# Moving the second plain pair of the two-stream FFN ahead of the operand sums, and dealing the modulation sums to other places

## The chip, the cores and the metric

The kernel runs on one core of one Trainium2 chip. The metric is device microseconds of one execution; lower is better. The time of the kernel before is 2478.84 us, the median of three runs (2477.21 to 2480.55).

## The reference

All data is fp32. A sequence of 256 rows of 1024 columns goes through a first block of two layers (a mixing stage, then a feed-forward network with a short convolution). Its output and a second sequence `ctx` of 256 rows then go through a second block of two layers. The part that the change touches is the half-step FFN of the second block, whose gain and shift come from a conditioning vector:

```
m  = (silu(cond) @ w_mod + b_mod).reshape(9, 1024)        # modulation: 9 rows of 1024
def ffn_half_step(s, m, i, norm_g, w_in, w_out):
    h  = rmsnorm(s, norm_g) * (1 + m[3*i+1]) + m[3*i]
    gu = h @ w_in                                         # 1024 x 5632
    y  = (silu(gu[:, :2816]) * gu[:, 2816:]) @ w_out      # 2816 x 1024
    return s + 0.5 * m[3*i+2] * y

for l in range(2):
    x, ctx = ffn_half_step(x, m_x, 0, ..), ffn_half_step(ctx, m_c, 0, ..)
    x, ctx = mixing stage over both
    x      = ffn_half_step(x, m_x, 2, ..)
    if l == 0:
        ctx = ffn_half_step(ctx, m_c, 2, ..)
```

So three times both streams pass through one FFN with the same weights (`ffn2s`: layer 0 step 0, layer 0 step 2, layer 1 step 0), and the last FFN works on x alone (`ffn2`).

## The kernel before, in words

**Products.** TensorE takes operands in a reduced-precision type, so each fp32 operand is split into a part `hi` (a cast on ScalarE, L303) and a part `lo` (the difference on VectorE, L304). A product then takes three matmuls, hi·hi, hi·lo, lo·hi (`mm3`, L308 to L310). Weights are split in the same way, as they arrive: `upraw` is the tile that the DMA fills, `upwhi` and `upwlo` are its two parts. A suffix in a tile's name is its phase: `f` is the first part of an FFN, `t` the operand sums, `up` the up projection, `dn` the down projection, `e` the last FFN, `lat`, `cv` and `wo` the mixing stage.

**Two-stream FFN, `ffn2s`.** The up projection makes 22 pairs (gate column block, up column block) for both streams. The first `NU` = 3 pairs are plain: `firsts` issues 24 matmuls for each of four results of a pair (two halves, two streams). They run on unnormalised rows; `plain` then reads the results out of PSUM, multiplies them by the row factor of each stream (`rooted`, L1088 and L1091), and applies Silu and the product (L1237, L1238). Pairs 3 and on take seven products in place of eight, in the manner of Strassen (`begin`, `middle`, `ends`). For those, `sums` builds the operands from the normalised rows of both streams: for each k of 0 to 3 it scales and normalises a row tile of x and one of ctx (L1119, L1120, L1122), forms four sums and differences (L1135, L1136, L1138, L1143) and splits all of them into hi and lo. The operands are called x1, x2, t1 to t4 and c2. `seven` loads the raw weights of a pair, adds them on DMA queues and on VectorE (L1164) and splits the four sums that it needs.

**PSUM.** There are three pools: `ps` with four banks, `sc` with two and `tp` with two. In the first part pair 0 takes three `ps` banks; pair 1 takes both `sc` banks and the fourth `ps` bank; pair 2 takes the three `ps` banks of pair 0 again. The first seven-product pair, j = 3, takes a `ps` bank for its first result (`upps`, W11·x1), one for W12·x2, and an `sc` bank for s1·t1 (`upsc`). So it needs banks that pair 1 held.

**Modulation sums.** `mod_step(n)` does up to n of a list of row sums that later stages need. Each is one pass of VectorE over 1024 columns (L473), and every second one first loads 512 KB of `w_mod` (tile `wm`, on SP's queue). Calls of it are spread through the loops over pairs j. What is left on the list is done where the next stage needs it (`mod_in`).

**What sets the order.** A scheduler orders the program on each engine by priority and readiness, and each engine then runs its instructions strictly in that order. `tc.issue_after(x)` orders what is written inside it behind x. Tile pools hand out buffers in rotation, so who frees a buffer also decides when a load starts. The lines that matter before:

```
        g0 = self.plain(first[0], Rs, gmore(0))
        self.phase = "t"
        self.sums(Rs, tmore)
        ...
                    g.append(self.plain(first[j], Rs_in, gmore(jj)) if j else g0)
        ...
                u = self.begin(a[wu][l, 2 * j], a[wu][l, 2 * j + 1])
                self.mod_step(1 + (n > 0 and jj % 2))
```

Pair 0 is read out of PSUM ahead of the sums, pairs 1 and 2 behind them.

Of the kernel before, what the change touches and what calls it, by code (L numbers as in the profile page):

```python
# [216 lines left out]
class Net:  # L217
# [740 lines left out]
    def ffn1(self, l, R):  # L958
# [9 lines left out]
        for j in range(KF):  # L968
            if j % 2 == 0:
                pair = self.r4(2, 2, T)  # L970
            us = []
            for i in range(2):
                if j:
                    ps = self.times(W if 2 * j + i == 2 else a["w1u"][l, 2 * j + i], h)
                else:
                    ps = self.f1()
                    nc.vector.tensor_tensor(ps, first[i], R, ALU.mult)  # L977
                if i == 0 and (j % 2 if l == 1 else j > 9):
                    self.mod_step(1, (0, 1, 16))
                c = KF * i + j  # L980
                u = self.f1()
                nc.scalar.activation(u, ps, AF.Identity, bias=self.c1(l, "fb", c), scale=self.c1(l, "fw", 44 + c))
                nc.vector.scalar_tensor_tensor(u[:, 1:T], ps[:, 0:T - 1], self.c1(l, "fw", c), u[:, 1:T],
                                               ALU.mult, ALU.add)
                nc.vector.scalar_tensor_tensor(u[:, 0:T - 1], ps[:, 1:T], self.c1(l, "fw", 88 + c), u[:, 0:T - 1],
                                               ALU.mult, ALU.add)
                us.append(u)
            s = self.f1()
            act = nc.scalar.activation(s, us[0], AF.Silu)
            if l == 0 and j == 8:  # L990
                with self.tc.issue_after(act.ins):
                    nc.scalar.activation(self.cond, self.cond, AF.Silu)
            nc.vector.tensor_tensor(s, s, us[1], ALU.mult)
            self.parts(pair[:, j % 2, 0, :], pair[:, j % 2, 1, :], s)
            g.append((pair[:, j % 2, 0, :], pair[:, j % 2, 1, :]))
# [112 lines left out]
    def sums(self, Rs, more):  # L1108
# [3 lines left out]
        self.B7 = {n: [] for n in ("x1", "x2", "c2", "t1", "t2", "t3", "t4")}  # L1112
        tiles = (self.r4(1024, more=m) for m in more)

        def h(s, k):

            f = self.f2().rearrange("p (a b) -> p a b", a=2)
# [13 lines left out]
        for k in range(4):  # L1131
# [9 lines left out]
                y = next(tiles).rearrange("p (a h b) -> p a h b", a=2, h=2)  # L1141
            t4 = self.f1()
            nc.vector.scalar_tensor_tensor(t4, c[:, 0], -1.0, x[:, 1], ALU.mult, ALU.subtract)  # L1143
            self.parts(y[:, k % 2, 0], y[:, k % 2, 1], t4)
            self.B7["t4"].append((y[:, k % 2, 0], y[:, k % 2, 1]))

    def seven(self, gate, up):
# [4 lines left out]
        s = self.t("es", [P, 1024], 2, pool=self.p_second).rearrange("p (a b) -> p a b", a=8)  # L1152
        W = {}

        def split(x, a, b=None):
            n = x.shape[1]
            hi, lo = [self.t(t, [P, 1024], 4, F32R)[:, :n * P].rearrange("p (a b) -> p a b", a=n)
                      for t in ("whi", "wlo")]
# [84 lines left out]
    def ffn2s(self, l, step, Rs, tmore, gmore, n4):  # L1243
# [6 lines left out]
        if self.mods and self.mods[0][3]:  # L1250

            self.mod_step(1)
        g0 = self.plain(first[0], Rs, gmore(0))
        self.phase = "t"
        self.sums(Rs, tmore)
        out = [{}, {}]
# [1 line left out]
        for n, (j0, j1) in enumerate(CHUNKS):  # L1258
            g, todo = [], []
            self.phase = "up"  # L1260
            for jj, j in enumerate(range(j0, j1)):
                if j < NU:
                    g.append(self.plain(first[j], Rs_in, gmore(jj)) if j else g0)
                    continue
                u = self.begin(a[wu][l, 2 * j], a[wu][l, 2 * j + 1])
                self.mod_step(1 + (n > 0 and jj % 2))
                if todo:
                    todo.pop(0)()
                self.middle(u, todo.pop(0) if todo else lambda: None)
# [36 lines left out]
    def ffn2(self, l, step, R, nh, ng):  # L1306
# [10 lines left out]
        for half in range(2):  # L1317
            g = []
            for jj in range(HF):
                j = half * HF + jj  # L1320
                if j >= nu:
                    pss = []
                    for i in range(2):
                        pss.append(self.times(W if 2 * j + i == 2 * nu else a[wu][l, 2 * j + i], h))
                        self.mod_step(1)
                s = self.f2()[:, :T]
                if j >= nu:
                    nc.scalar.activation(s, pss[0], AF.Silu)
# [369 lines left out]
    def body(self):  # L1698
# [18 lines left out]
        with tc.tile_pool(name="second", bufs=1) as big:  # L1717
# [6 lines left out]
            for l in range(LAYERS):  # L1724
                self.next = two("w2i", l)

                if l == 0:
                    Rs = self.ffn2s(l, 0, Rs, [False] * 14, lambda jj: jj > 0, 8)
                else:
                    Rs = self.ffn2s(l, 0, Rs, [i >= 7 for i in range(14)], lambda jj: jj == 0, 8)  # L1730
                self.next = two("w2u2", l)
                Rs = self.mix2(l, Rs)
                if l == 0:
# [28 lines left out]
```

## Time and profile before

| what | before |
|---|---|
| median of three runs | 2478.84 us |
| the profiled execution | 2478.33 us |
| its span on the core | 2476.4 us, mean granted clock 0.99 |
| TensorE matmul busy | 2405.1 us, 97% of the span |
| VectorE busy | 2081.4 us, 84% |
| ScalarE busy | 1407.3 us, 57% |

The busy share is a mean over all stages. The gap of 1.9 us between the profiled execution and its span lies outside the records. Times in the views count from the start of the span. In a timeline a row is one instruction, or several of one kind run together (x2, x4): start, time until the last one's end, engine, line, operation, tiles, and in brackets the idle time ahead of it with what ended it. Matmuls overlap, so that the distance of two starts, and not the listed duration, is what one matmul takes.

### The profile page before, as it was taken

What the parts mean: (1) busy time and instruction counts of PE and PEld (TensorE: products, weight loads), DVE (VectorE), ACT (ScalarE), POOL (GpSimd) and SP (SyncE); (2) the same over time, 40 slices, a digit from 0 to 9 for tenths busy, and PEclk for the clock granted to TensorE, in tenths of its full rate; (3) what the DMA queues carried; (4) which work ended last, traced back from release to release, by engine and by line L of the source; (5) the groups of instructions that cost most, each with busy time, mean ns of one, the idle gap of its engine ahead of it and who ended that gap; (6) DMA issues with size and microseconds to landing.
All of it is one profiled execution on the core that took longest, in us unless ns stands there. A gap on an engine that the chain in (4) does not pass through costs nothing.

```text
span 2476.4 us, 45471 instructions
## 1 busy us (share of the span) xinstructions
PE 2405.1 (97%) x17419; PEld 2240.9 (90%) x17419; DVE 2081.4 (84%) x3779; ACT 1407.3 (57%) x2529; POOL 100.0 (4%) x128
## 2 busy tenths in 40 slices
PE   8999999999999989999999989999989999999998
PEld 7999999899899988989887888989888989888998
DVE  7888997988999787889877788888888889888754
ACT  7766665756665563535536673535563535667444
POOL 0000000000000000100000000101010101000000
PEclk9999999999999999999999999999989999999999
DMA  7545667545676556777331347777447778434664
GB/s 250 171 154 181 214 215 259 179 157 166 219 227 212 173 137 196 198 206 205 121 107 35 117 128 211 185 216 205 152 108 208 199 232 247 135 110 155 217 206 122
DMA packets 145195, 441.68 MB, mean 178 GB/s; under 512 B 16720, under 2 KB 19536, under 8 KB 144720
## 3 DMA queue, kind: packets, MB, share of 16 engines
q1 hardware_dynamic: 128560, 408.88, 51.0%
q0 software_dynamic: 16416, 29.89, 7.4%
q8 instruction: 137, 2.24, 0.4%
q14 instruction: 82, 0.67, 0.1%
HBM read 437.66 MB, written 1.05 MB: 177 GB/s over the span
## 4 chain that ended last, share of the span: by engine, by line
PE 79%; DVE 10%; DMA 5%; ACT 3%; issue 2%; SPq 0%; DVEq 0%; ACTq 0%; POOLq 0%
PE upps L310 7%; PE upps L308 7%; PE upps L309 7%; PE dnps L308 6%; PE dnps L310 6%; PE dnps L309 6%; DMA upes<-in_w2u 3%; DVE upwlo L304 2%; PE eps L308 2%; PE eps L310 2%; PE eps L309 2%; PE upsc L308 1%; PE upsc L309 1%; PE upsc L310 1%; DVE upjunk L473 1%
## 5 line engine op out<-in xcount | busy, mean ns | idle before, releaser
L303 ACT CAST upwhi<-upraw 128x1024 fp32r<-128x1024 f32 (+1 forms) x253 | 241.0, 953 | 199.6 <-PE upps L309 82.7
L304 DVE TENSOR_TENSOR upwlo<-upraw,upwhi 128x1024 fp32r<-128x1024 f32 (+1 forms) x253 | 274.3, 1100 | 26.9 <-ACT upwhi L303 25.2
L310 PE MATMUL upps<-tr,upwlo 128*128 128x256 f32 x931 | 264.6, 284 | 10.5 <-DVE upwlo L304 10.3
L308 PE MATMUL upps<-tr,upwhi 128*128 128x256 f32 x931 | 265.1, 285 | 0.9 <-ACT upf L1202 0.9
L309 PE MATMUL upps<-tr,upwhi 128*128 128x256 f32 x931 | 263.9, 284 | 0.0
L303 ACT CAST dnwhi<-dnraw 128x896 fp32r<-128x896 f32 (+3 forms) x146 | 130.8, 897 | 205.1 <-PE dnps L309 145.8
L310 PEld LDWEIGHTS upps<-tr,upwlo 128*128 128x128 f32 x931 | 178.1, 191 | 12.5 <-DVE upwlo L304 12.5
L310 PE MATMUL upps<-hr,upwlo 128*128 128x256 f32 x656 | 184.5, 282 | 1.2 <-DVE upwlo L304 1.1
L308 PE MATMUL upps<-hr,upwhi 128*128 128x256 f32 x656 | 185.0, 282 | 0.2 <-DVE upf L977 0.2
L309 PE MATMUL upps<-hr,upwhi 128*128 128x256 f32 x656 | 185.1, 282 | 0.0
L308 PEld LDWEIGHTS upps<-tr,upwhi 128*128 128x128 f32 x931 | 178.2, 191 | 4.4 <-ACT upf L1208 3.0
L309 PEld LDWEIGHTS upps<-tr,upwhi 128*128 128x128 f32 x931 | 178.1, 191 | 0.3
L304 DVE TENSOR_TENSOR dnwlo<-dnraw,dnwhi 128x896 fp32r<-128x896 f32 (+3 forms) x146 | 150.1, 1030 | 23.6 <-ACT dnwhi L303 22.8
L310 PE MATMUL dnps<-upr,dnwlo 128*128 128x256 f32 (+1 forms) x535 | 169.6, 317 | 0.0
L308 PE MATMUL dnps<-upr,dnwhi 128*128 128x256 f32 (+1 forms) x535 | 169.4, 317 | 0.0
L309 PE MATMUL dnps<-upr,dnwhi 128*128 128x256 f32 (+1 forms) x535 | 169.2, 316 | 0.0
L473 DVE SCALAR_TENSOR_TENSOR dnjunk<-dnwm,cond 128x1024 bf16<-128x1024 f32 x117 | 142.4, 1217 | 2.8 <-DMA dnwm<-in_wm 2.5
L310 PE MATMUL dnps<-upr4b,dnwlo 128*128 128x512 f32 (+1 forms) x342 | 132.1, 387 | 0.0
L308 PE MATMUL upsc<-tr,upwhi 128*128 128x256 f32 x361 | 102.2, 283 | 30.4 <-DVE upf L1091 30.4
L308 PE MATMUL dnps<-upr4b,dnwhi 128*128 128x512 f32 (+1 forms) x342 | 131.4, 385 | 0.0
L309 PE MATMUL dnps<-upr4b,dnwhi 128*128 128x512 f32 (+1 forms) x342 | 131.3, 384 | 0.0
L310 PEld LDWEIGHTS upps<-hr,upwlo 128*128 128x128 f32 x656 | 124.5, 190 | 2.0 <-DVE upwlo L304 1.9
(876 smaller groups left out, 8333.8 us busy)
## 6 DMA issues: line engine op xcount, KB each, us to landing
upraw<-in_w2u SPq DMA_DIRECT2D x114, 512.0 KB, 4.7
upraw<-in_w1u SPq DMA_DIRECT2D x82, 512.0 KB, 4.3
dnwm<-in_wm SPq DMA_DIRECT2D x69, 512.0 KB, 4.5
upwm<-in_wm SPq DMA_DIRECT2D x56, 512.0 KB, 5.1
dnraw<-in_w2d SPq DMA_DIRECT2D x48, 448.0 KB, 4.2
eraw<-in_w2u SPq DMA_DIRECT2D x42, 512.0 KB, 4.4
upes<-in_w2u SPq DMA_DIRECT2D x57, 256.0 KB, 3.1
upes<-in_w2u POOLq DMA_DIRECT2D x57, 256.0 KB, 6.1
```

The source lines that it names most:

```text
L303: act = self.nc.scalar.copy(hi, src)
L304: return act, self.nc.vector.tensor_tensor(lo, src, hi, ALU.subtract)
L308: mm(ps, L[0], R[0], start=st, stop=False, skip_group_check=skip)
L309: mm(ps, L[0], R[1], start=False, stop=False, skip_group_check=skip)
L310: mm(ps, L[1], R[0], start=False, stop=sp, skip_group_check=skip)
L473: nc.vector.scalar_tensor_tensor(junk, self.wm, 1.0, self.cond[:, s, :], ALU.mult, ALU.mult, accum_out=self.M[l][s][step][:, j:j + 1])
```

## The change

Four edits. First, pair 1 is read out of PSUM with pair 0, ahead of the sums; only pair 2 stays behind them. Second, `sums` notes the splits of its t4 operands in `self.order`, and the first `seven` after it orders its weight splits behind them: the split of W11 and W12 behind k = 0, the other three behind k = 2. Third, modulation sums are taken out of the first pairs of several loops; the list is done in the same sequence, so they come later. Counted from the programs of both kernels, in the first block's second FFN the steps go from 11 to 12 and start at pair 5, not at pair 1; each `ffn2s` has 3 of them in its loop over pairs where it had 5; the mixing stage of layer 0 has 12 in its `cv` part where it had 11 and 1 in `wo` where it had none; the mixing stage of layer 1 has 2 in `lat` where it had 1, and 3 in `cv` where it had none; the last FFN keeps 8, from a later pair. Fourth, flags say from which of two tile pools some operand buffers come.

```
@@ first block's FFN
-                if i == 0 and (j % 2 if l == 1 else j > 9):
+                if i == 0 and (j > 3 and (j % 2 or j > 15) if l == 1 else j > 9):
                     self.mod_step(1, (0, 1, 16))
@@ sums
+        self.order = []
...
-            self.parts(y[:, k % 2, 0], y[:, k % 2, 1], t4)
+            self.order.append(self.parts(y[:, k % 2, 0], y[:, k % 2, 1], t4))
@@ seven
+        late = [self.order[0], self.order[2]] if self.order else []
+        self.order = []
+
         def split(x, a, b=None):
+            if late:
+                act, dve = late[a != "11"]
+                with self.tc.issue_after(act.ins), self.tc.issue_after(dve.ins):
+                    cut(x, a, b)
+            else:
+                cut(x, a, b)
+
+        def cut(x, a, b):
@@ ffn2s
-        g0 = self.plain(first[0], Rs, gmore(0))
+        g0 = [self.plain(first[j], Rs, gmore(j)) for j in range(2)]
         self.phase = "t"
         self.sums(Rs, tmore)
...
-                    g.append(self.plain(first[j], Rs_in, gmore(jj)) if j else g0)
+                    g.append(self.plain(first[j], Rs_in, gmore(jj)) if j > 1 else g0[j])
                     continue
                 u = self.begin(a[wu][l, 2 * j], a[wu][l, 2 * j + 1])
-                self.mod_step(1 + (n > 0 and jj % 2))
+                if j > NU + 1:
+                    self.mod_step(1 + (n > 0 and jj % 2))
@@ ffn2
-                        self.mod_step(1)
+                        if j > nu + 1:
+                            self.mod_step(1)
@@ calls of ffn2s, step 0
-                    Rs = self.ffn2s(l, 0, Rs, [False] * 14, lambda jj: jj > 0, 8)
+                    Rs = self.ffn2s(l, 0, Rs, [i == 13 for i in range(14)], lambda jj: jj > 1, 8)
-                    Rs = self.ffn2s(l, 0, Rs, [i >= 7 for i in range(14)], lambda jj: jj == 0, 8)
+                    Rs = self.ffn2s(l, 0, Rs, [7 <= i < 13 for i in range(14)], lambda jj: jj < 2, 8)
```

**VectorE where the sums begin, first `ffn2s`.** Before, in the order of VectorE's program (`ff` is a plain pair's result, `fsc` and `fps` are PSUM banks, `dnR` and `qkvRc` the row factors of x and ctx, `tf` a row tile of the sums and `tr` its split parts):

```order
L1238 SCALAR_TENSOR_TENSOR ff21890_11258<-ff21891_11259,fbs1892_11260,ff21890_11258 128x256
L1088 COPY upbs1926_11394<-fsc1871_11034 128x2
L1164 TENSOR_TENSOR upes1955_11532<-upes1955_11532,upraw1953_11528 128x512
L304 TENSOR_TENSOR fr41893_11271<-ff21890_11258,fr41893_11271 128x512
L1120 TENSOR_TENSOR tf21895_11280<-tf21895_11280,qkvRc1017_5842 128x512
L304 TENSOR_TENSOR tr41896_11286<-tf21894_11274,tr41896_11286 128x512
L304 TENSOR_TENSOR upwlo1936_11430<-upraw1932_11424,upwhi1935_11429 128x1024
L1135 TENSOR_TENSOR tf21897_11289<-tf21894_11274,tf21895_11280 128x256
```

The same place in the changed kernel, from the row behind pair 0's split `fr41893` (its lines are numbered up to 13 higher here):

```order
L1088 COPY fbs1896_11276<-fsc1872_11036 128x2
L1091 TENSOR_TENSOR ff21894_11274<-fsc1872_11036,dnR2561868_10932 128x256
L1088 COPY fbs1896_11276<-fsc1873_11037 128x2
L1091 TENSOR_TENSOR ff21895_11275<-fsc1873_11037,dnR2561868_10932 128x256
L1251 SCALAR_TENSOR_TENSOR ff21894_11274<-ff21895_11275,fbs1896_11276,ff21894_11274 128x256
L1122 TENSOR_TENSOR tf21898_11290<-tf21898_11290,dnR2561868_10932 128x512
L1091 TENSOR_TENSOR ff21894_11274<-fps1874_11038,qkvRc1017_5842 128x256
L1091 TENSOR_TENSOR ff21895_11275<-fps1874_11038,qkvRc1017_5842 128x256
L1251 SCALAR_TENSOR_TENSOR ff21894_11274<-ff21895_11275,fbs1896_11276,ff21894_11274 128x256
L304 TENSOR_TENSOR fr41897_11287<-ff21894_11274,fr41897_11287 128x512
L1088 COPY upbs1930_11410<-fps1881_11147 128x2
L1122 TENSOR_TENSOR tf21899_11296<-tf21899_11296,qkvRc1017_5842 128x512
```

The reads of pair 1's three banks (`fsc1872`, `fsc1873`, `fps1874`) and one read of pair 2's first bank (`fps1881`) now stand between pair 0's split and the normalised ctx row of k = 0 (L1120 before, L1122 now), and the first weight split `upwlo1936` no longer stands there.

**TensorE behind the plain pairs, same place.** Before:

```order
L310 MATMUL fps1882_11147<-dnr4b1842_10789,fwlo1888_11205 128x256
L308 MATMUL upsc1950_11499<-tr41898_11292,upwhi1937_11437 128x256
L309 MATMUL upsc1950_11499<-tr41898_11292,upwhi1937_11437 128x256
L310 MATMUL upsc1950_11499<-tr41898_11292,upwlo1938_11438 128x256
L308 MATMUL upsc1950_11499<-tr41906_11322,upwhi1937_11437 128x256
L309 MATMUL upsc1950_11499<-tr41906_11322,upwhi1937_11437 128x256
L308 MATMUL upps1943_11450<-tr41896_11286,upwhi1935_11429 128x256
```

Now, the last rows of W11·x1 and the first of s1·t1:

```order
L308 MATMUL upps1943_11450<-tr41923_11391,upwhi1935_11429 128x256
L309 MATMUL upps1943_11450<-tr41923_11391,upwhi1935_11429 128x256
L310 MATMUL upps1943_11450<-tr41923_11391,upwlo1936_11430 128x256
L308 MATMUL upsc1948_11495<-tr41902_11308,upwhi1937_11437 128x256
L309 MATMUL upsc1948_11495<-tr41902_11308,upwhi1937_11437 128x256
L310 MATMUL upsc1948_11495<-tr41902_11308,upwlo1938_11438 128x256
```

Before, s1·t1 came first; now all of W11·x1 comes first (12 matmuls, the last three on the split x row of k = 3), then s1·t1 (12), s2·t2 (12), W12·x2 (12) and s3·t3 (12).

**VectorE in the mixing stage of layer 1.** Before, from the first to the second of the weight splits of its convolution part:

```order
L304 TENSOR_TENSOR cvwlo4364_25652<-cvraw4362_25649,cvwhi4363_25651 128x1024
L1397 SCALAR_TENSOR_TENSOR latf24316_25451<-latr44303_25369,p2_469,latf24315_25446 128x512
L1397 SCALAR_TENSOR_TENSOR latf24318_25456<-latr44303_25369,p2_469,latf24315_25446 128x512
L321 TENSOR_TENSOR latS2564332_25534<-latS2564332_25534,latnq4333_25536 128x256
L1437 TENSOR_TENSOR latf24320_25461<-latps4307_25385,latr4b4272_25190 64x512
L304 TENSOR_TENSOR latr44317_25453<-latf24316_25451,latr44317_25453 128x512
L304 TENSOR_TENSOR latr44319_25458<-latf24318_25456,latr44319_25458 128x512
L1438 TENSOR_TENSOR latf24321_25462<-latps4307_25385,latr4b4272_25190 64x512
L304 TENSOR_TENSOR cvwlo4368_25683<-cvraw4366_25680,cvwhi4367_25682 128x1024
```

Now, the last rows up to the second split, the first of which stands ten rows behind the first split:

```order
L473 SCALAR_TENSOR_TENSOR cvjunk4363_25674,M102_138<-cvwm4362_25672,cond_471 128x1024
L1458 TENSOR_TENSOR latr4b4314_25450<-latf24312_25445,latr4b4314_25450 64x512
L1458 TENSOR_TENSOR latr4b4315_25451<-latf24312_25445,latr4b4315_25451 64x512
L304 TENSOR_TENSOR latr44340_25598<-latps4336_25566,latr44340_25598 128x256
L344 SCALAR_TENSOR_TENSOR latnq4343_25605<-lattp4341_25601,latnq4342_25604 128x256
L304 TENSOR_TENSOR cves4354_25632<-cvraw4355_25633,cvr4b4353_25631 128x1024
L345 TENSOR_TENSOR latnq4343_25605<-latnq4343_25605,latnq4342_25604 128x256
L304 TENSOR_TENSOR cvwlo4366_25679<-cvraw4364_25676,cvwhi4365_25678 128x1024
```

Between the two splits stand 16 instructions where there were 7, two modulation sums (L473) among them.

## Rows read from the trace of the kernel before

**Rows 1.** The page, part 1: busy time, share of the span, instructions.
```profile
span 2476.4 us, 45471 instructions
...
PE 2405.1 (97%) x17419; PEld 2240.9 (90%) x17419; DVE 2081.4 (84%) x3779; ACT 1407.3 (57%) x2529; POOL 100.0 (4%) x128
```

**Rows 2.** Waits: engine, line, who is waited for: us in total, times, longest.
```profile
PE upsc L308 <- DVE upf L1091: 30.4, 3, 10.2
```

**Rows 3.** Timeline of TensorE, first two-stream FFN, end of the plain pairs.
```profile
862.87 0.28 PE L308 MATMUL fps<-dnr4b,fwhi 128*128 128x258 f32 x1
...
865.77 0.28 PE L308 MATMUL fps<-dnr4b,fwhi 128*128 128x256 f32 x1
...
884.65 0.55 PE L308 MATMUL upsc<-tr,upwhi 128*128 128x256 f32 x1 [10.17 <-DVE upf L1091]
...
893.60 0.28 PE L310 MATMUL upps<-tr,upwlo 128*128 128x256 f32 x1
```

**Rows 4.** Windows: busy time by engine, granted TensorE clock, DMA share and GB/s.
```profile
874.40:884.60 10.20, 0.08 (x1) 0.00 (x0) 10.06 (x22) 7.12 (x16) 0.86 (x1) 0.71 0.21 67
886.00:888.00 2.00, 2.00 (x12) 2.00 (x11) 1.98 (x6) 1.03 (x2) 0.00 (x0) 0.50 0.33 58
892.00:896.00 4.00, 4.00 (x36) 4.00 (x35) 2.98 (x4) 1.93 (x4) 0.00 (x0) 1.00 0.07 14
```

**Rows 5.** Timeline of VectorE, same place: first and last of the sums.
```profile
857.02 0.68 DVE L1120 TENSOR_TENSOR tf<-tf,qkvRc 128x512 f32<-128x512 f32 x1
...
876.80 0.69 DVE L1120 TENSOR_TENSOR tf<-tf,dnR 128x512 f32<-128x512 f32 x1
877.40 0.68 DVE L1164 TENSOR_TENSOR upes<-upes,upraw 128x512 f32<-128x512 f32 x1
878.01 0.69 DVE L1120 TENSOR_TENSOR tf<-tf,qkvRc 128x512 f32<-128x512 f32 x1
...
879.21 1.22 DVE L473 SCALAR_TENSOR_TENSOR upjunk<-upwm,cond 128x1024 bf16<-128x1024 f32 x1
...
880.35 0.69 DVE L304 TENSOR_TENSOR tr<-tf,tr 128x512 fp32r<-128x512 f32 x1
880.96 0.42 DVE L1135 TENSOR_TENSOR tf<-tf,tf 128x256 f32<-128x256 f32 x1
...
882.55 1.62 DVE L304 TENSOR_TENSOR tr<-tf,tr 128x512 fp32r<-128x512 f32 x3
884.09 0.74 DVE L1091 TENSOR_TENSOR upf<-fsc,dnR 128x256 f32<-128x256 f32 x2
```

**Rows 6.** Timeline of ScalarE, same place.
```profile
875.81 0.90 ACT L1119 ACTIVATE tf<-xs,dnMA 128x256 f32<-128x256 f32 x2
876.62 0.89 ACT L1119 ACTIVATE tf<-cs,dnMA 128x256 f32<-128x256 f32 x2
877.42 0.60 ACT L303 CAST upwhi<-upraw 128x512 fp32r<-128x512 f32 x1
```

**Rows 7.** Timelines of VectorE and TensorE, second FFN of the first block.
```profile
653.71 1.21 DVE L473 SCALAR_TENSOR_TENSOR upjunk<-upwm,cond 128x1024 bf16<-128x1024 f32 x1
...
655.32 0.39 PE L309 MATMUL upps<-hr,hwhi 128*128 128x256 f32 x1 [1.04 <-DVE hr L304]
```

**Rows 8.** Timelines of VectorE, ScalarE and TensorE, last FFN.
```profile
2293.17 1.22 DVE L473 SCALAR_TENSOR_TENSOR ejunk<-ewm,cond 128x1024 bf16<-128x1024 f32 x1
...
2300.84 1.04 ACT L303 CAST ewhi<-eraw 128x1024 fp32r<-128x1024 f32 x1 [2.33 <-DMA eraw<-in_w2u]
...
2301.94 0.58 PE L308 MATMUL eps<-er,ewhi 128*128 128x256 f32 x1 [2.37 <-ACT ewhi L303]
```

**Rows 9.** Timelines of VectorE and TensorE, mixing stage of layer 1.
```profile
2170.69 1.23 DVE L304 TENSOR_TENSOR cvwlo<-cvraw,cvwhi 128x1024 fp32r<-128x1024 f32 x1 [0.23 <-ACT cvwhi L303]
...
2176.38 1.23 DVE L304 TENSOR_TENSOR cvwlo<-cvraw,cvwhi 128x1024 fp32r<-128x1024 f32 x1
...
2181.94 1.21 DVE L304 TENSOR_TENSOR cves<-cvraw,cvr4b 128x1024 fp32r<-128x1024 f32 x1
...
2181.51 0.28 PE L310 MATMUL cvps<-latr,cvwlo 128*128 128x256 f32 x1
```

**Rows 10.** Windows, mixing stage of layer 1 (columns as in rows 4).
```profile
2170.00:2180.00 10.00, 10.00 (x85) 9.89 (x84) 9.56 (x14) 6.23 (x12) 0.00 (x0) 1.00 0.42 139
```

## The prediction

> **What bounds the kernel now.** The page's first part comes first [rows 1]: TensorE's matmuls fill 97% of the span, VectorE 84%, ScalarE 57%. So most of the time TensorE is the bound, and only two things move the end: what makes TensorE idle, and what makes it run at half clock. The list of waits is read next [rows 2]: one wait stands out, of TensorE on VectorE's reads of a plain pair (L1091), three times, 30.4 us in all. TensorE's timeline shows one of them [rows 3]: the last plain results end at about 874.5 (the first two of pair 2's four groups of 24 start at 862.87 and 865.77, so that one takes 2.9 us, and three from 865.77 on end there), then nothing runs until 884.65. The window over that gap shows VectorE busy for 10.06 of 10.20 us, and ScalarE for 7.12 [rows 4]: the operand sums are made there. TensorE comes back at a granted clock of 0.50, the 1.2 GHz level, and 12 matmuls in 2 us (20 in all, 0.21 us each); from 889 on it has 1.00, and 36 matmuls take 4 us [rows 4]. The 60 matmuls of the first five products end at 893.7 [rows 3]. The other stalls are ten times smaller; those that the change touches are 1.04 us in the first block [rows 7] and 2.37 us in the last FFN [rows 8].
>
> **The plain pair ahead of the sums, three times.** VectorE runs in the written order, so what counts is when the sums start and how long they take. Before, the ctx row of k = 0 is normalised at 857.02 [rows 5], and the sums end at 884.09. Now pair 1's three banks are read first, and behind them the first bank of pair 2 (`fps1881`), all ahead of that row. TensorE's own order there is unchanged, and pair 2's first group starts at 862.87 and ends when the next group starts, at 865.77, or one matmul's tail later, 865.9 [rows 3]. So the row cannot start before 866.0: 9.0 us later than now, and VectorE has little else to do in between, as the weight split that filled such gaps is ordered behind k = 0.
>
> How long the sums take: in the last block of them the two normalisations take 0.60 each by their distance to the next row, the first split 0.61 (880.35 to 880.96), the four sums 1.59 (880.96 to 882.55), the other splits 1.54 (to 884.09) [rows 5], together 4.94; four blocks without the x row that is already done are 19.2. Between them stand three weight splits of 1024 columns and one of 512, 1.14 and 0.60 (a modulation sum of the same width is started 1.14 ahead of its successor [rows 5]), and one L1164 at 0.61 [rows 5]: 4.6. The modulation sum at 879.21 [rows 5] is gone. Work without a wait is 23.8, so 889.8. But every split needs ScalarE's cast first, and every row ScalarE's two scalings (0.81 a pair, a cast of 512 columns 0.51 [rows 6]). Walking both programs row by row with these durations, VectorE waits 3.8 us, and the sums end at 893.6 (the split x row of k = 3 at 887, t1 of k = 3 at 891.3).
>
> Against that, TensorE no longer has 60 matmuls to do after the sums. It does W11·x1 as the rows come, s1·t1 to 892, then s2·t2 to 895.2 at half clock (0.21 each), W12·x2 to 896.7 and s3·t3 to 898.1 at full clock. Before, the five products ended at 893.7 [rows 3]. **Price: +4.4 us a stage.** Lower bound: no wait of VectorE and full clock. The sums end at 889.8 and 27 matmuls of 0.12 follow, 892.9, so about −1.0 with the last operand a little ahead. Upper bound: all 27 at 0.21 behind 893.3, and half a microsecond for two copies out of PSUM between them, which is a choice: 899.6, +5.9. I take +4.4, the walk. The wait stands in the list three times with 10.14 to 10.2 us [rows 2], so three stages of one shape: **+13.2** (−3 to +17.7).
>
> The Trainium skill speaks for the change here: "Perfetto Trace Analysis", section on identifying performance opportunities, says that the same gap repeating on the engine that should be saturated can mean that PSUM or SBUF lacks room for the next tile. By that rule freeing pair 1's banks would close the gap, and the sum would be that of the faster rival below; rows 5 show VectorE making operands until the gap's end.
>
> **The modulation sums.** *First block, second FFN.* The sum at 653.71 stood ahead of the split that TensorE waited 1.04 us for [rows 7]; it goes to a later pair, where TensorE does not wait. One such stall, and part of the next ones behind the same queue: **−1.5** (0 to −2.5, if a weight split takes its place or if all small stalls there go). *Last FFN.* The sum at 2293.17 leaves, and with it a load on SP's queue ahead of the weights; the cast at 2300.84 waited 2.33 us for its DMA, and TensorE 2.37 us for the cast [rows 8]. The load itself starts when a weight tile comes free, some 0.5 us sooner: **−0.8** (0 to −2.4). *Mixing stage of layer 0.* One sum more, beside a TensorE that does not wait on VectorE there: 0 (0 to +1.1). *The two-stream loops.* The sums left out there stood behind TensorE's work and make no stall of their own beside the one above: 0.
>
> *Mixing stage of layer 1.* Here four sums are added, each of 1.14 us, and VectorE has no room: 9.56 us of 10 [rows 10]. The second weight split of the convolution part starts at 2176.38, is done at 2177.5, and TensorE needs it at 2181.51 [rows 9], 4 us of slack. Now the sum added in `lat` (1.14), two more (2.28) and eight rows that used to come later stand ahead of it, among them the split that was at 2181.94 [rows 9], 1.13 and the rest 0.33 to 0.65: some 3.9 us, less the 0.3 that VectorE waited. So 2177.5 becomes 2184.5, a wait of 3.0; the third split is a further sum late, +1.0. **+4** (0, if the order of TensorE leaves it other work, to +5.3).
>
> Sum: 13.2 − 1.5 − 0.8 + 4 = +14.9 on the profiled execution's 2478.33 (span 2476.4), that is **2493**; the median of the runs, 2478.84, is 0.5 above that execution, which changes nothing.
>
> **Rivals.**
> *Head start and delay cancel.* The sums end 6 to 7 us later, but TensorE has 33 of 60 matmuls behind it by then and is at full clock. This needs VectorE to wait about 1.3 us as before, not 3.8: each stage −0.5 to +1.5, and with the other terms 2478 to 2483. For it: ScalarE is busy for only 7.12 of 10.20 us in the gap [rows 4]. Against: without the weight splits between them the rows of a block follow each other directly through both engines.
> *Faster: the gap closes.* If the ctx row of k = 0 does not wait for pair 2's bank, reading out pair 1 costs VectorE 2.7 us (two pairs of reads at 0.7 [rows 5], two products of 0.4 and a split of 0.6), the sums start at 859.7, end at 884 to 887, and TensorE has done most of its 60 matmuls by then: 4 to 6 us gained in each stage, 15 in all, with the terms of the modulation sums 2465. It decides when that row starts before 861.6 (866.0 less 4.4). For it: nothing but the copy of two columns of `fps1881` holds the row back. Against: the copy is in the written order.
> *The modulation sums decide alone*, the plain pairs being neutral: +1.7, within the first rival.
>
> **How the numbers follow.** Three runs of this kernel spread by 0.13%, so 0.2%, about 5 us, is about what a measurement can tell from no change. Chances: slower as forecast 0.65 (own range 2484 to 2501: stages between +2 and +5.9 with the mixing stage between +1 and +5), cancelling 0.20 (2474 to 2484), faster 0.15 (2460 to 2473). The range takes the first two whole and the edge of the third: 2472 to 2502.
>
> **What would show it.** In the changed trace the ctx row of k = 0 in the first two-stream FFN starts at 866.0 if the delay is right, at 861.6 or before if the faster rival is; TensorE then idles in several pieces behind the plain pairs, released by splits of the sums (`tr`) and weight splits, not by L1091, and 60 matmuls end at 898 (893.7 before). The list of waits loses its row of 30.4 us and gains rows of TensorE on VectorE's `tr` and `upwlo` of 40 us or so in all. The stall at 655.32 is gone, that at 2301.94 smaller, and a wait on `cvwlo` of 3 us is there at about 2185 (shifted by what came before). The prediction is wrong if the sums run with fewer waits than walked, if TensorE's clock stays at 1.00 through the pieces, or if the wait of the convolution part finds other work.

## The result, and the profile after

The changed kernel takes 2499.07 us (median of four runs, 2498.3 to 2501.49), the kernel before 2478.03 us in the same comparison (four runs, 2468.56 to 2480.55). The ratio is 1.0087, with a 95% interval of 1.0065 to 1.0109: 21 us slower, where 2493 was forecast. The profiled execution took 2501.49 us, its span 2499.6, 23.2 more than the span of before.

The page's first part hardly shows it:

```profile
span 2499.6 us, 45444 instructions
...
PE 2421.1 (97%) x17419; PEld 2250.7 (90%) x17419; DVE 2080.9 (83%) x3779; ACT 1407.4 (56%) x2529; POOL 99.9 (4%) x128
```

TensorE is busy for 16 us longer with the same 17419 matmuls [rows 1], so part of the loss is matmuls that take longer, not idle time. The list of waits tells where the rest is. Its row of 30.4 us [rows 2] is gone, and these have come up or grown:

```profile
DVE upes L1177 <- DMA upes<-in_w2u: 36.4, 18, 4.2
...
PE upps L310 <- DVE upwlo L304: 19.1, 13, 2.7
...
PE upps L308 <- ACT tr L303: 16.9, 4, 5.1
...
PE upps L308 <- ACT tr4b L303: 8.5, 2, 5.1
```

Two of the four are in the list of before too, and smaller (L1164 there is L1177 here):

```profile
DVE upes L1164 <- DMA upes<-in_w2u: 22.7, 17, 2.9
...
PE upps L310 <- DVE upwlo L304: 11.4, 11, 2.4
```

TensorE no longer waits for a PSUM bank to be read. It waits for the operands themselves, the split row tiles `tr` and `tr4b` of the sums, six times for 25.4 us. Its timeline at the place of [rows 3] shows two of them, then the end of the five products, and one stall more:

```profile
877.50 0.58 PE L308 MATMUL upps<-tr,upwhi 128*128 128x256 f32 x1 [5.14 <-ACT tr L303]
...
882.62 0.58 PE L308 MATMUL upps<-tr,upwhi 128*128 128x256 f32 x1 [3.31 <-ACT tr L303]
...
894.70 0.28 PE L310 MATMUL upps<-tr,upwlo 128*128 128x256 f32 x1
...
897.86 0.39 PE L310 MATMUL upps<-tr,upwlo 128*128 128x256 f32 x1 [2.17 <-DVE upwlo L304]
```

VectorE's timeline at the place of [rows 5] holds the cause of each. The first four rows are the reads of pair 1 and the copy from pair 2's first bank, the fifth is the ctx row of k = 0, the sixth the end of the sums, the seventh an add that VectorE waits 4.14 us for, the last the weight split behind it:

```profile
856.99 0.16 DVE L1088 COPY fbs<-fsc 128x2 f32<-128x2 f32 x1 [3.23 <-PE fsc L310]
...
859.82 0.76 DVE L1091 TENSOR_TENSOR ff<-fps,qkvRc 128x256 f32<-128x256 f32 x2 [0.80 <-PE fps L310]
...
861.99 0.69 DVE L304 TENSOR_TENSOR fr<-ff,fr 128x512 fp32r<-128x512 f32 x1 [0.69 <-ACT fr L303]
862.71 0.16 DVE L1088 COPY upbs<-fps 128x2 f32<-128x2 f32 x1
862.80 0.69 DVE L1122 TENSOR_TENSOR tf<-tf,qkvRc 128x512 f32<-128x512 f32 x1
...
889.31 0.75 DVE L1091 TENSOR_TENSOR upf<-fps,dnR 128x256 f32<-128x256 f32 x2
...
895.25 0.69 DVE L1177 TENSOR_TENSOR upes<-upes,upraw 128x512 f32<-128x512 f32 x1 [4.14 <-DMA upes<-in_w2u]
...
896.59 1.22 DVE L304 TENSOR_TENSOR upwlo<-upraw,upwhi 128x1024 fp32r<-128x1024 f32 x1
```

So the sums start late because VectorE stands in front of pair 1's banks until TensorE has filled them: it waits 3.23 us for the second and 0.80 us for the third, and then for ScalarE's cast of the pair. The copy from pair 2's first bank follows without a wait that the list shows.

And the windows, with the columns of [rows 4], give the clock of those pieces:

```profile
871.50:877.40 5.90, 0.71 (x4) 0.30 (x2) 5.14 (x11) 5.22 (x12) 0.00 (x0) 0.86 0.00 0
878.50:882.60 4.10, 0.80 (x2) 0.50 (x2) 3.03 (x6) 3.55 (x10) 0.00 (x0) 0.50 0.00 0
889.00:891.00 2.00, 2.00 (x11) 2.00 (x11) 2.00 (x7) 0.51 (x1) 0.00 (x0) 0.50 0.80 156
891.00:893.00 2.00, 2.00 (x12) 2.00 (x11) 0.11 (x1) 1.49 (x3) 0.00 (x0) 0.54 1.03 271
898.00:902.00 4.00, 4.00 (x34) 4.00 (x35) 3.33 (x6) 1.90 (x4) 0.00 (x0) 1.00 0.32 65
```

**Where the 23 us are.** The same matmul can be looked up in both traces, and the difference of its two starts (after less before) tells how far the program has fallen behind there. Where this difference changes, time is lost or won:

| stretch (times of before) | difference at its start and end | change |
|---|---|---|
| up to 650 | 0 to +0.3 | +0.3 |
| first block's second FFN, 650 to 690 | +0.3 to -3.3 | -3.6 |
| two-stream FFN 1, plain pairs to second pair of sevens, 860 to 900 | -3.3 to +3.5 | +6.8 |
| rest of it and mixing stage, to 1440 | +3.5 to -1.1 | -4.6 |
| two-stream FFN 2, same place | -1.1 to +5.9 | +6.9 |
| rest of it | +5.9 to +10.2 | +4.3 |
| two-stream FFN 3, same place | +10.2 to +16.4 | +6.3 |
| rest of it, to 2160 | +16.4 to +21.4 | +5.0 |
| mixing stage of layer 1, to 2290 | +21.4 to +26.8 | +5.4 |
| last FFN, 2290 to 2330 | +26.8 to +22.0 | -4.8 |
| to the end | +22.0 to +22.9 | +0.9 |

The three places of the pair cost 20.0 us. Of the 16 us that TensorE is busy for longer, 14.2 lie in them too (860 to 900, 1440 to 1480 and 1800 to 1838 of before, and the same matmuls in the changed kernel: 87.6 and 101.8 us). The table is of one execution each; executions of before alone lay between 2468 and 2488 us in the experiments, so single entries below 2 us are not read as more than that.

### The profile page after: what moved, and what is told of

Its sections match the earlier page's. It is cut to its first block, busy times and chain, and to the rows that moved or that the text cites. A ratio compares the mean times of both kernels' runs of the same rounds, so it can differ in the third digit from the quotient of the medians.

```text
span 2499.6 us, 45444 instructions
## 1 busy us (share of the span) xinstructions
PE 2421.1 (97%) x17419; PEld 2250.7 (90%) x17419; DVE 2080.9 (83%) x3779; ACT 1407.4 (56%) x2529; POOL 99.9 (4%) x128
## 4 chain that ended last, share of the span: by engine, by line
PE 81%; DVE 8%; DMA 5%; ACT 3%; issue 2%; SPq 0%; DVEq 0%; ACTq 0%; POOLq 0%
PE upps L310 7%; PE upps L308 7%; PE upps L309 7%; PE dnps L310 7%; PE dnps L308 7%; PE dnps L309 6%; DMA upes<-in_w2u 4%; PE eps L308 2%; PE eps L309 2%; PE eps L310 2%; DVE upwlo L304 2%; PE upsc L308 1%; PE upsc L309 1%; PE upsc L310 1%; PE qkvps L309 1%
## 5 line engine op out<-in xcount | busy, mean ns | idle before, releaser
L308 PE MATMUL upps<-tr,upwhi 128*128 128x256 f32 x931 | 268.5, 288 | 18.8 <-ACT tr L303 16.9
L309 PE MATMUL upps<-tr,upwhi 128*128 128x256 f32 x931 | 266.9, 287 | 2.2 <-DVE tr L304 2.2
L308 PE MATMUL dnps<-upr,dnwhi 128*128 128x256 f32 (+1 forms) x527 | 166.2, 315 | 0.0
L309 PE MATMUL dnps<-upr,dnwhi 128*128 128x256 f32 (+1 forms) x527 | 166.1, 315 | 0.0
L473 DVE SCALAR_TENSOR_TENSOR dnjunk<-dnwm,cond 128x1024 bf16<-128x1024 f32 x118 | 143.5, 1216 | 3.5 <-DMA dnwm<-in_wm 3.5
L310 PE MATMUL dnps<-upr4b,dnwlo 128*128 128x512 f32 (+1 forms) x326 | 125.7, 386 | 0.0
L308 PE MATMUL dnps<-upr4b,dnwhi 128*128 128x512 f32 (+1 forms) x326 | 125.3, 385 | 0.0
L309 PE MATMUL dnps<-upr4b,dnwhi 128*128 128x512 f32 (+1 forms) x326 | 125.0, 384 | 0.0
L308 PEld LDWEIGHTS upps<-hr,upwhi 128*128 128x128 f32 x656 | 123.6, 188 | 1.1 <-ACT upwhi L303 1.1
```

The source lines that it names most:

```text
L308: mm(ps, L[0], R[0], start=st, stop=False, skip_group_check=skip)
L309: mm(ps, L[0], R[1], start=False, stop=False, skip_group_check=skip)
L310: mm(ps, L[1], R[0], start=False, stop=sp, skip_group_check=skip)
L473: nc.vector.scalar_tensor_tensor(junk, self.wm, 1.0, self.cond[:, s, :], ALU.mult, ALU.mult, accum_out=self.M[l][s][step][:, j:j + 1])
```

## The experiments

**Theory.** Reading pair 1 ahead of the sums makes them start 9 us later, and TensorE, which gets its operands from them, cannot win that back. **Rivals:** the modulation sums make the loss; the order of the weight splits makes it; or the sums' end sets the time whatever is ahead. The change has three parts that can stand alone: the pair (P), the order of the weight splits (O) and the modulation sums (M). All eight combinations have a time. The flags of the fourth edit go with the pair, as before where the pair is as before. Ratios are to the kernel before, in runs on the same chip. What a place costs is read from one execution of each run, as in the table.

**P and O, without M.** The modulation sums go back to where they stood:

```
-                if j > NU + 1:
-                    self.mod_step(1 + (n > 0 and jj % 2))
+                self.mod_step(1 + (n > 0 and jj % 2))
```

(and the same for the conditions in the two other loops.)

> The pair and the order of the weight splits as changed, the modulation sums where they stood before. Theory (the plain pair delays the sums): the three two-stream FFNs lose 6.5 us each up to the second product of pair 4, as in the changed kernel's trace (+4.1 until the fifth product of pair 3, +2.4 at the next weight split), so +19.5: 2497 us (2492 to 2503), and the wait of 2.4 us on a weight split in the mixing stage of layer 1 is gone. Rival (the modulation sums decide): within 3 us of before, 2475 to 2481.

Measured: 2494.24 us, ratio 1.0077 (1.0061 to 1.0094). The loss is the pair's and the order's, the rival is out. The three places cost 4.8, 5.4 and 3.9 us, less than in the changed kernel, and VectorE shows why. A modulation sum stands where the waiting add stood, and the weight split, with no wait for a DMA ahead of it, comes at 897.4 by the clock of before (this execution is 2.3 us ahead there), where the changed kernel has it at 899.9:

```profile
891.99 1.22 DVE L473 SCALAR_TENSOR_TENSOR upjunk<-upwm,cond 128x1024 bf16<-128x1024 f32 x1
...
895.09 1.22 DVE L304 TENSOR_TENSOR upwlo<-upraw,upwhi 128x1024 fp32r<-128x1024 f32 x1
```

**M alone.** The changed kernel with the pair read as before and the list of splits to wait for emptied:

```
-        g0 = [self.plain(first[j], Rs, gmore(j)) for j in range(2)]
+        g0 = self.plain(first[0], Rs, gmore(0))
...
-                    g.append(self.plain(first[j], Rs_in, gmore(jj)) if j > 1 else g0[j])
+                    g.append(self.plain(first[j], Rs_in, gmore(jj)) if j else g0)
...
-        late = [self.order[0], self.order[2]] if self.order else []
+        late = []
```

> The modulation sums as changed, the pair and the weight splits as before. Theory: -3.3 us in the first block's second FFN, -3.5 us in the last FFN, +4.8 us in the mixing stage of layer 1, all three read from the changed kernel's trace, together -2.0: 2476 us, with 4 us to either side for what the sums do in the later part of the loops over pairs. The three gaps of 10.1 us stay. Rival (the modulation sums are the loss): 2493 us or more.

Measured: 2468.68 us, ratio 0.9968 (0.9955 to 0.9981): faster, and more than expected. The mixing stage of layer 1 loses as much as in the changed kernel (5.6 us), the last FFN gains 5.4. What the expectation left out is that the gap itself shrinks:

```profile
879.83 0.55 PE L308 MATMUL upsc<-tr,upwhi 128*128 128x256 f32 x1 [8.58 <-DVE upf L1091]
```

8.58 us where it was 10.17 [rows 3], for a modulation sum of 1.14 us that no longer stands among the operand sums (879.21 in [rows 5]). VectorE's work in that stretch sets the gap. The other two gaps are 8.7 us here, and though pair 1 is still read behind the sums, they are put down to the operands and not to its bank:

```profile
PE upsc L308 <- ACT tr L303: 8.7, 1, 8.7
PE upsc L308 <- ACT tr4b L303: 8.7, 1, 8.7
```

**P alone.** The list of splits to wait for is emptied, and the modulation sums stand where they did:

```
-        late = [self.order[0], self.order[2]] if self.order else []
+        late = []
...
-                if j > NU + 1:
-                    self.mod_step(1 + (n > 0 and jj % 2))
+                self.mod_step(1 + (n > 0 and jj % 2))
```

> The pair ahead of the sums, the weight splits not ordered behind the sums, the modulation sums as before. Theory: the ctx row of k = 0 still stands behind pair 1's reads and starts about 9 us later than before; but the weight tiles come free early, so that the wait of 2.2 us on the next pair's weight split at 897.86 is gone: +4 a stage, 2490 us (2484 to 2496). Rival (the order of the weight splits is the whole loss): 2478 us or less.

Measured: 2492.33 us, ratio 1.0065 (1.0041 to 1.009). As the theory had it; the rival (the order is the whole loss) is out. The three places cost 3.2, 4.1 and 4.0 us.

**The pair inside the sums.** Pair 1 is read behind the block of k = 0, without O and M:

```
-        g0 = [self.plain(first[j], Rs, gmore(j)) for j in range(2)]
+        g0 = [self.plain(first[0], Rs, gmore(0))]
...
-        self.sums(Rs, tmore)
+        self.sums(Rs, tmore, lambda: g0.append(self.plain(first[1], Rs, gmore(1))))
... in sums, behind the block of k:
+            if k == 0:
+                then()
```

> Pair 1 read out inside the sums, behind the block of k = 0; weight splits and modulation sums as before. Theory: the ctx row of k = 0 starts where it did before (857.0), the sums end about 1 to 2 us later than before, since 2.7 us of reads stand between them, and TensorE has some 40 of the 60 matmuls behind it by then: -4 to -5 us a stage, 2465 us (2460 to 2472). Rival (the sums' end sets the time, whatever is done ahead of it): the stage ends 1 to 3 us later than before, 2480 to 2487 us.

Measured: 2480.7 us, ratio 1.0012 (0.9996 to 1.0027): no difference that can be measured. The loss is gone, so the late start of the sums was it (and not the flags, which are as changed here): the ctx row of k = 0 is at 854.00, which is 856.9 on the clock of before (this execution is 2.9 us ahead there), against 857.02 [rows 5] and 866.1 in the changed kernel. But the gain of 4 to 5 us a place did not come either; by the time the rival came out (2480 to 2487), not the theory. The rival's reason holds only in part: the sums end 2.5 us later than before (886.6 for 884.09, on the clock of before), and yet the places win 1.2, 0.6 and 1.0 us in the profiled execution, which was the fastest of the twelve (2471.09 us). TensorE's timeline and windows show where it went:

```profile
880.81 0.58 PE L308 MATMUL upps<-tr,upwhi 128*128 128x256 f32 x1 [3.95 <-ACT tr L303]
```

```profile
874.00:880.00 6.00, 2.12 (x6) 1.40 (x6) 6.00 (x12) 5.11 (x12) 0.00 (x0) 0.59 0.16 46
880.00:884.00 4.00, 3.00 (x11) 2.48 (x12) 4.00 (x12) 2.67 (x6) 0.86 (x1) 0.50 0.25 70
```

The banks are free, but TensorE still waits for each block of the sums, and what it does in the pieces it does at a granted clock of 0.50 to 0.59. VectorE is busy for 10.0 of 10 us: the reads of pair 1 now stand inside the sums.

**O alone.** The weight splits wait for the sums; the pair is read as before:

```
-        g0 = [self.plain(first[j], Rs, gmore(j)) for j in range(2)]
+        g0 = self.plain(first[0], Rs, gmore(0))
...
-                if j > NU + 1:
-                    self.mod_step(1 + (n > 0 and jj % 2))
+                self.mod_step(1 + (n > 0 and jj % 2))
```

> Only the order of the weight splits behind the sums, pair and modulation sums as before. Theory (the splits' order has two sides): two splits of 1.14 us and one of 0.60 leave the stretch of the sums, so pair 1's bank is read some 2.5 us sooner and the gap of 10.1 us shrinks to about 7.5; the tile of the weight sum comes free late, so a DMA of a later pair lands late and VectorE waits for it, which gives 1 to 2.5 us back: 0 to -1.5 a stage, 2473 to 2477 us. Rival (the order alone costs what the extra wait showed, 2.4 us a stage): 2484 us.

(The flags and the conditions in the two other loops are as before too.)

Measured: 2474.86 us, ratio 0.9974 (0.9957 to 0.999): as expected by the time. The order is not harmful by itself; the wait for the pair's bank comes to 25.7 us over the three places:

```profile
PE upsc L308 <- DVE upf L1091: 25.7, 3, 10.3
```

The gap shrinks as expected in the first and the third of them (7.74 and 7.68 us), but not in the second (10.30 us), where three of the weight splits still stand among the sums. The places win 2.8, lose 0.9 and win 2.4 us.

**P and M, without O.** In the changed kernel:

```
-        late = [self.order[0], self.order[2]] if self.order else []
+        late = []
```

> The changed kernel without the order of the weight splits: pair 1 ahead of the sums and the modulation sums as changed. Theory: the wait of 2.2 us on the next pair's weight split goes (the DMA of the weight sum starts some 18 us earlier), while the late start of the sums stays: 2.4 to 3 us less a stage than the changed kernel, so 2489 to 2492 us. Rival (the late DMA is a consequence of the late sums and not of the order): 2499 us.

Measured: 2490.47 us, ratio 1.0048 (1.0033 to 1.0063), so some 9 us better than the changed kernel. VectorE's wait of 4 us for the add is not there; the places cost 5.9, 4.9 and 5.9 us, 0.4 to 2.0 less than with O, and more is won between them.

**The weight sum's split alone out of the order.** In the changed kernel:

```
-            if late:
+            if late and a != "s2":
```

> The changed kernel, with the split of the weight sum (s2, s1) alone taken out of the order behind k = 2; everything else on VectorE stays in its place, the add of pair 5 ahead of the split of pair 4 too. Theory (the tile of the weight sum comes free late, its DMA lands late, VectorE waits 4.1 us for it in front of a split that TensorE needs): that wait and TensorE's 2.2 us behind it go in the three two-stream FFNs, 1.5 to 2.4 us each: 2492 to 2495 us. Rival (the wait is there whenever pair 1 goes first): 2499 us.

Measured: 2489.62 us, ratio 1.0046 (1.0031 to 1.0061): 9.5 us less than the changed kernel, 2.4 us beyond the range expected. The add is in the same place of VectorE's program and waits for nothing:

```profile
891.14 0.68 DVE L1177 TENSOR_TENSOR upes<-upes,upraw 128x512 f32<-128x512 f32 x1
```

and its load starts 11.8 us earlier. On SP's queue it stands at 872.98 in this run, 884.80 in the changed kernel and 866.05 before, in this order:

```profile
872.98 0.33 SPq L1180 DMA_DIRECT2D upes<-in_w2u  x1
```

```profile
884.80 0.33 SPq L1180 DMA_DIRECT2D upes<-in_w2u  x1
```

```profile
866.05 0.33 SPq L1167 DMA_DIRECT2D upes<-in_w2u  x1
```

The load fills the tile that the split of pair 3 has just read (that split runs from 883.55 in the changed kernel), so ordering the split late makes the load late, and with it the add, and everything queued behind the add. The three places cost 4.8, 5.2 and 4.4 us, 1.7 to 2.0 less each; this is the second part of the loss there. It is less than the wait of 4.14 us, since VectorE now waits 1.72 us for W11·x1 behind the add. The rest of the 9.5 us was won outside the places, and no run isolates where.

**O and M, without P.** In the changed kernel:

```
-        g0 = [self.plain(first[j], Rs, gmore(j)) for j in range(2)]
+        g0 = self.plain(first[0], Rs, gmore(0))
```

> The order of the weight splits and the modulation sums as changed, the pair as before: the last corner of the eight. Theory (the parts are not additive, since the order already takes a modulation sum out of the stretch of the sums, and without the sums an add that waits for a DMA comes ahead of a split): not -3 - 8.4 = -11.4 but -4 to -8: 2470 to 2474 us, about the run with the modulation sums alone. Rival (additive): 2466 us or less.

Measured: 2467.64 us, ratio 0.995 (0.9935 to 0.9966). 11 us faster than before, and faster than the 2470 to 2474 us expected. O and M as they are alone would multiply to 0.9942, within the interval, so that over the whole run no departure from additive is shown. At the three places there is one: they win 2.2, lose 0.7 and win 2.6 us, no more than with O alone.

With this the eight corners are: before 1; P 1.0065; O 0.9974; M 0.9968; P and O 1.0077; P and M 1.0048; O and M 0.995; all three 1.0087. With P and without it, all else equal, the ratio differs by 0.0065, 0.0103, 0.0080 and 0.0137: the pair is the loss in each case, and most in company with both others. The order costs something only in company with the pair: 0.0012 without M, where the intervals overlap, and 0.0039 with it.

**Two tries for a faster version.** Four more modulation sums in the last down projection, so that none is left for the convolution part of the mixing stage:

```
-                    self.mod_step(2 if d < 6 else 1)
+                    self.mod_step(2 if d < 6 or l == 1 else 1)
```

> The modulation sums as changed, pair and weight splits as before, and in the last two-stream FFN four more modulation sums in the down projection, so that the mixing stage of layer 1 gets one in its first part and none in its convolution part, as before. Theory: the wait of about 5 us there goes, on top of the 8 us that the modulation sums gave: 2464 us (2460 to 2468). Rival (the four sums only move the wait into the down projection): 2469 us.

Measured: 2469.74 us, ratio 0.9966 (0.9951 to 0.9981), no better than M alone: the rival's time. The mixing stage lost nothing now (0.6 us in place of 5), but in the loop before it the difference grew by some 6 us, above all at a stall of TensorE of 3.19 us in the up projection, behind an add that waits 3.15 us for its weights. More modulation sums there mean more loads of 512 KB on the queue that brings the weights (nine of them between 1995 and 2025, where M alone has six); that these make the weights late is read from the queue and not isolated by a run. The same with the pair behind k = 0:

```
-        self.sums(Rs, tmore)
+        self.sums(Rs, tmore, lambda: g0.append(self.plain(first[1], Rs, gmore(1))))
```

> As the run with four more modulation sums in the last down projection, and pair 1 read behind the block of k = 0. Theory (VectorE's work on the sums sets the end of the gap, and products done ahead run at half clock): no more than 1 us a stage on top of that run, 2460 to 2465 us. Rival (with a modulation sum less in the stretch TensorE gets through more of the 60 matmuls): 3 us a stage on top, 2455 us.

Measured: 2471.02 us, ratio 0.997 (0.9954 to 0.9985). No gain on top, as the theory had it, though above its 2460 to 2465 us, as the run that it builds on was.

**A sum less moved.** Of the two modulation sums that M takes out of each first chunk, only that of pair 3, again without P and O:

```
-                if j > NU + 1:
+                if j > NU:
                     self.mod_step(1 + (n > 0 and jj % 2))
```

> The modulation sums as changed, but in the two-stream FFNs only the one of pair 3 left out, not that of pair 4; pair and order as before. Theory (what counts in these FFNs is the one sum that stands among the operand sums): the three gaps shrink as in the run with all modulation sums moved (10.1 to about 8.6 us), and with fewer sums in the mixing stage of layer 1 its wait is smaller: 2467 to 2472 us. Rival (the sum of pair 4 carries half of the gain): 2473 us or more, the gaps as before.

Measured: 2466.31 us, ratio 0.9944 (0.9925 to 0.9963), the fastest version of all by its median, though its interval overlaps that of M alone. The gap is the same as in the run with both moved:

```profile
880.20 0.55 PE L308 MATMUL upsc<-tr,upwhi 128*128 128x256 f32 x1 [8.65 <-DVE upf L1091]
```

So the sum of pair 3 carried what M gains there, and the sum of pair 4 carried nothing.

## Why the prediction was right, and where its sizes were off

*What bounds the stretch: right.* The prediction read the gap as VectorE and ScalarE making operands, and not as PSUM. Freeing the banks turned the wait for L1091 into waits for `tr`, and the run with the banks free and the sums on time gained nothing that can be measured. The Trainium skill ("Perfetto Trace Analysis", section on identifying performance opportunities) says that a repeated gap *can* mean a lack of PSUM; here the named wait was a bank, and the lack was of operands, which the busy columns of [rows 4] told.

*The sums start 9 us later: right in size, half right in its reason.* Forecast 866.0; measured 862.80 in an execution that is 3.3 us ahead there, 866.1 by the clock of before. The prediction had only pair 2's first bank hold the row back. But pair 1's own last bank is full no sooner than pair 2's first group starts, at 862.87 [rows 3]; VectorE reads it at 859.82, which is 863.1 by the clock of before, and the split of the pair ends at 862.68, just ahead of the copy. So the row could not have started at the faster rival's 859.7 even without pair 2's bank, and that both limits lie at 866 is luck. The sums ended at 889.31, or 892.6 (forecast 893.6, so some 1 us less waiting than walked, the first of its signs of being wrong, in part), and the 60th matmul of the five products started at 894.70, or 898.0 (forecast end 898.1). **Price of this step: +4.4 forecast; the start of s3·t3 moved from 3.3 us ahead to 1.1 us behind, which is 4.4.**

*What the sum lacked.* The walk stopped at the fifth product. Behind it stands the next weight split, queued behind an add whose load the new order of the splits had made late: 2.4 us more in the first place (from +1.1 to +3.5). The diff's second edit had been costed only by what it moves inside the sums, not by when its tiles come free. That term was not in the sum: 6.8, 6.9 and 6.3 measured for 4.4, all above the upper bound of 5.9, and 20.0 for 13.2. Two runs show it: without the order, and with only the weight sum out of it, the add does not wait. (The rows of 40 us or so that the prediction expected for `tr` and `upwlo` came to 44.5, with the `tr` rows put down to ScalarE's casts; but 11.4 us of the `upwlo` row were there before.)

*Why P, O and M are worse together.* In the corner with P and O a modulation sum stands ahead of the split where the changed kernel has the add. And O by itself already takes a modulation sum out of the stretch of the sums, since the sums' place is tied to the last split; M cannot win there a second time, as the places of the run with O and M show. So two edits that are gains alone do not help the third. This is read from the orders and traces; the part of it on the add is shown by the run with the weight sum free. In the corner with P and M, without O, the places still cost 4.9 to 5.9 us with no wait for the add, and no run says why that is more than the walk's 4.4.

*Modulation sums.* Mixing stage of layer 1: +4 forecast, +5.4 measured up to the last FFN; the four runs with the modulation sums of before show +1.1 to +1.5 over the same stretch, so about +4.1 is the change's. The wait itself was forecast at 3.0 and is

```profile
2206.78 0.43 PE L310 MATMUL cvps<-latr,cvwlo 128*128 128x256 f32 x1 [2.36 <-DVE cvwlo L304]
```

and the matmuls behind it run at half clock for a while (16 of them bring the difference from +25.0 to +26.6). Last FFN: -0.8 forecast, -4.8 measured: the stall of 2.37 us [rows 8] and one of 1.25 are gone with the half clock behind them, where the prediction had counted a part of one. The four runs with the sums of before show -2.1 to +1.4 there and all the others with them moved -5.1 to -5.9, so that at least 2.6 us are the change's. First block: -1.5 forecast, -3.6 in the table. But the four runs with the modulation sums where they stood are also 2.0 to 2.4 us faster there than the profiled execution of before, and five of the eight runs with them moved no more than that, so that between nothing and 1.6 us is the change's. The two-stream loops: 0 forecast; M alone shows -2.0, -1.4 and -1.9 at the three gaps, for the sum at 879.21, which the prediction had booked in its walk (23.8 us of work without it) and nowhere else.

*What stays open.* The rests of the three loops, -4.6, +4.3 and +5.0 us, forecast at nothing. The stalls there (up to 2.67 us) stand behind adds that wait up to 3.9 us for their loads, and in the run with the weight sum free the same rests are -1.9, 0.0 and -2.0. Which load is late there depends on the whole of what went before, and no run isolates it. Executions of before alone differ by 0.8%, where the prediction had taken 0.2% for what a measurement can tell.

*How near the sum came.* Its +14.9 stands against 22.9 in the table. The three places are 6.8 us above it, the mixing stage 1.4 and what it had at nothing 5.9; the first block is 2.1 us below it and the last FFN 4.0. That the errors set each other off in part, and that the time lies within the range, is luck; the sign and the largest term are not.

The rivals: the one in which delay and head start cancel (2478 to 2483) is wrong here, as VectorE waited 2.7 us in the sums (862.80 to 889.31, less 23.8 of work) and not 1.3. The faster one (2465) is wrong in its mechanism too: its condition could not hold, and in the nearest run, with the sums on time and the pair read inside them, the places win 0.6 to 1.2 us, not 4 to 6. The third, that the modulation sums decide alone (+1.7), is out by M alone, which was faster.

## What to carry to other kernels

A wait names the last thing that was missing, not the scarce thing: before freeing the resource that a stall names, look at which engine is busy through the stall, and ask whether the freed engine would have operands. When work is put ahead of a producer on an in-order engine, find out when that work's own inputs are ready, since the engine will stand in front of it until then; price the producer's delay against the consumer's head start, and remember that a head start in pieces may run at half clock. When a read of a buffer is ordered later, follow the buffer: the load that reuses it, the instruction that waits for that load, and what is queued behind it.

## What the runs showed of the hardware

Matmuls done in pieces, between waits of 3 to 5 us, ran at half clock here: in the changed kernel the granted clock was 0.50 from 878.5 to 882.6, still 0.50 from 889 to 891 with TensorE busy all the time, and 1.00 from 898 to 902. Before, one gap of 10.2 us was followed by some 20 matmuls at half clock [rows 3, 4]; here 39 start from 877.50 to 892.8, between and behind the gaps of 5.1 and 3.3 us. In two traces with the same 17419 matmuls TensorE's busy time differs by 16 us; not all of that is the clock, as a matmul alone behind a wait is listed with 0.58 us (877.50, 882.62). And the spread of executions of one kernel, 2468 to 2488 us, was wider than the 0.13% of its first three runs.
